# Expert numbers by steps, one-hots with stored pairs, and modulation vectors spread over the mixer's last stages

## The chip, the cores and the metric

The kernel runs on one core of one Trainium2 chip. The metric is the device time of one execution in microseconds (us), the median of several runs. All inputs and outputs lie in the chip's memory. One launch computes the whole trunk.

## The reference, cut to what matters

512 tokens of 1024 numbers pass through two layers. Each layer has a mixer (a gated linear recurrence HGRN2 in 8 heads beside a state space model S5, merged by gates) and an expert half, PEER. Both halves are entered through an RMS norm that is shifted and scaled by modulation vectors, and left through a modulated residual. All weights are float32.

```python
c_act = jax.nn.silu(c)
for l in range(DEPTH):                                   # 2
    mod = c_act @ ada_w[l] + ada_b[l]                    # 6 vectors of 1024
    sh1, sc1, g1, sh2, sc2, g2 = jnp.split(mod, 6, axis=-1)
    proj = modulate(rms_norm(x, norm1_g[l]), sh1, sc1) @ w_in[l]
    # q, f, i, og -> y_a (HGRN2); u -> y_s (S5, gelu); ga, gb: gates
    y_b = y_s * jax.nn.sigmoid(y_s @ glu_w[l] + glu_b[l])
    merged = jax.nn.sigmoid(ga) * y_a + jax.nn.sigmoid(gb) * y_b
    x = x + g1 * (merged @ w_out[l])
    h2 = modulate(rms_norm(x, norm2_g[l]), sh2, sc2)
    x = x + g2 * peer_layer(h2, ...)

# peer_layer, for every token and each of 8 heads:
s = jnp.einsum('thpd,hpnd->thpn', q, keys32)             # p = 2 halves, n = 128 keys
s1_v, s1_i = top_k(s[:, :, 0], 16); s2_v, s2_i = top_k(s[:, :, 1], 16)
cand_v = s1_v[..., :, None] + s2_v[..., None, :]         # 16 x 16 pairs
cand_i = s1_i[..., :, None] * 128 + s2_i[..., None, :]
top_v, top_j = top_k(cand_v, 16)
idx = take_along_axis(cand_i, top_j)                     # numbers of 16 experts of 16384
gate = softmax(top_v)
act = gelu(sum_d u_tab[idx] * h)                         # one dot product per chosen expert
out = sum_k gate * act * v_tab[idx]
```

## The kernel before

The activations lie transposed, `xT` [128, 8, 512]: channels on the partitions, tokens along the row. The order of the instructions on each engine is not the order of the text: a planner places every instruction by a priority (its place in the text, less an offset where a block asks for one) and by its own estimate of when operands and buffers are ready.

**A dense product** (`dense`, L125) multiplies 128 output channels by all tokens. Weight and activation are each split into a high part in TensorE's reduced float32 and the rest. `load_split` (L106) loads 512 KB on SP's queue into `raw` (4 buffers), ScalarE copies the high part `whi` (L114), VectorE subtracts to get `wlo` (L116), and 24 matmuls follow: 8 depth blocks times high-high (L132), high-low (L133) and low-high (L134). Activations are split once per stage by `split_act` (L119, VectorE's part L123). Weight splits of later products are put up to 1000 places ahead (`HP`).

**The mixer's last stages** (L727 to L777) are 32 dense products: 8 gates for the S5 branch (`gates`, two and then six), 8 gates for the HGRN2 branch (win columns 40 to 47), 8 products with `glu`, and 8 with `wout`, the last three of them in two halves of 256 tokens (`dense_halves`). Among them the modulation vectors are computed: `ada` (L160) takes chunks of 128 outputs; each is one load of 512 KB on SP into a tile with two buffers and one VectorE product with accumulation (L165), and one VectorE sum per call adds the bias. There are 48 chunks per layer. Of a layer's own chunks 16 to 47, one stands after each of the eight win stages (`later(1)`) and three before each glu stage (`later(3)`); before the first five wout stages of layer 0 stand chunks 0 to 15 of layer 1, four at a time (`later(4)`). `cond` loads c and computes its silu, in layer 1 just after the six gates.

**The expert half** (`peer`). `wq` gives 16 score blocks: `scores` (L812) copies the query, multiplies by the keys (L819, plain float32, 128x128) and takes the top 16 on VectorE. `select(tb)` (L826) works on a block of 128 tokens, one token per partition. It makes 50 candidate sums per head, those of the 16 x 16 pairs that can be among the top 16, with as many candidate numbers `ci`, and takes the top 16 and their positions `tj`. Then, for each of the 8 x 16 picks, one VectorE instruction (L855) compares a row of 0 to 49 with the position, multiplies by `ci` and accumulates the one number that is left; a shift and a mask split that number into the two key numbers `fx[0]` and `fx[1]`. The softmax gate is `fx[2]`.

The last 128 tokens fetch their experts one by one: `gather_steps` (L938) issues 128 indirect gathers of rows of U on POOL, with one VectorE dot product each (L946), and 128 of V, each added to `gacc` (L957), through three buffers `gr`.

The other 384 tokens use dense products over all 16384 experts. `dense_U` (L785) is a product with 128 experts, 24 matmuls of 384 columns, its gelu stored to memory; there are 128 per layer. The gate weights come from `build` (L886): for each token two matmuls (one for each part of the gate) of one-hot matrices [128 picks, 128 keys] puts the gates at their places in a 128 x 128 table. `select` transposes `fx` to picks on partitions and stores the two key numbers as float16 in `st` (`slot`) and the gate as a float16 high part and rest in `gh`, both with two buffers. One build takes 4 tokens: VectorE compares `io4` (a key number repeated four times) with four tokens' first and second key numbers (L900, L902), multiplies the second one-hot with the gate's two parts (L906, twice), all as [128, 128, 4] with the token as the innermost index; 8 matmuls follow (L912, L913), whose operands step over four elements; ScalarE copies to `stg` (L914), and every 12 builds `stg` goes to memory (`sW`).

```
    TE.matmul(ps[:, k], P_[:, :, t], Qs[0][:, :, t], start=True, stop=False)
    TE.matmul(ps[:, k], P_[:, :, t], Qs[1][:, :, t], start=False, stop=True)
```

In the text `select(3)` is first, then for each block of 0 to 2 its `select` and 32 builds, with one `dense_U` and one gather step after every second build, then the 80 remaining `dense_U` with a gather step each. After them comes the stage of V: for each of 128 groups of experts the stored gelu times the reloaded gates (L1007), a split (L1009, L1011), and 24 matmuls (L1020 to L1022) into eight accumulators, with the remaining gather steps between.

## Time and profile before

| what | value |
|---|---|
| median of three runs | 3928.33 us (3924.42 to 3931.42) |
| profiled execution's own time | 3930.45 us |
| its span | 3928.7 us, 62542 instructions |
| PE (TensorE) busy | 3736.3 us, 95% |
| PEld (weight loads, beside PE) | 3502.1 us, 89% |
| DVE (VectorE) busy | 3238.6 us, 82% |
| ACT (ScalarE) busy | 1574.6 us, 40% |
| POOL (GpSimd) busy | 1021.7 us, 26% |
| mean granted clock of TensorE | 0.97 |
| moved by DMA | 911.37 MB, 232 GB/s on the mean |

The span is the profiled part of one execution; 1.75 us lie around it. In time, layer 0's mixer heads take the first 450 us, the mixer's last stages 455 to 612, the score stage ends at 752, U and the builds run to 1435, V to 1965; layer 1 repeats this to the end. Busy shares are means over these stages. Clock and share are told as a part of one (1.00 is 2.4 GHz, 0.50 is 1.2 GHz). In a row, "out<-in" names the tiles written and read, and an arrow "<-" behind a wait names what ended it.

### The profile page before, as it was taken

To read this page: it belongs to the slowest core of one execution; us is meant where nothing else is said; L and a number is where in the kernel's file an instruction comes from. 1 tells how busy PE (TensorE), PEld (TensorE's weight loads), DVE (VectorE), ACT (ScalarE), POOL (GpSimd) and SP (SyncE) were. 2 spreads that over 40 slices of the span, in tenths; PEclk is the share of its full clock that TensorE was granted. 3 is DMA by queue.
4 is the path that set the end of the run, shared out by engine and by line. 5 is a ranking of instruction groups with operands and counts; after the bars stand their busy time and mean duration, and the time that the engine had idled before them with its cause. 6 is when DMAs were issued, how large, how long until landed. Compare 5 with 4: busy or idle time off the path is not lost.

```text
span 3928.7 us, 62542 instructions
## 1 busy us (share of the span) xinstructions
PE 3736.3 (95%) x21878; PEld 3502.1 (89%) x21878; DVE 3238.6 (82%) x8715; ACT 1574.6 (40%) x2507; POOL 1021.7 (26%) x1475
## 2 busy tenths in 40 slices
PE   6999999999999959999999999999999997699998
PEld 5888878999999959999988887789999997699998
DVE  6998787999898879877578886679998888787874
ACT  3554443333343323333345554344333433233332
POOL 7454100013222344221033440000232223432210
PEclk9999999999999969999999999999999998899999
DMA  5222384379998989998622225524898898999984
GB/s 197 74 64 78 102 266 143 111 249 318 326 315 304 322 300 351 348 344 315 208 85 75 71 81 168 187 84 136 303 309 315 310 325 289 333 353 344 347 294 134
DMA packets 368764, 911.37 MB, mean 232 GB/s; under 512 B 35824, under 2 KB 187440, under 8 KB 368448
## 3 DMA queue, kind: packets, MB, share of 16 engines
q1 hardware_dynamic: 247696, 536.56, 40.6%
q0 software_dynamic: 73952, 268.56, 19.7%
q10 hardware_dynamic: 46800, 102.26, 6.8%
q8 instruction: 172, 2.82, 0.3%
q14 instruction: 144, 1.18, 0.1%
HBM read 796.09 MB, written 111.15 MB: 231 GB/s over the span
## 4 chain that ended last, share of the span: by engine, by line
PE 77%; DVE 11%; DMA 7%; POOL 2%; issue 2%; ACT 1%; SPq 0%; ACTq 0%; DVEq 0%; POOLq 0%
PE mm L132 12%; PE mm L133 12%; PE mm L134 12%; PE mm L1021 3%; PE mm L1020 3%; PE mm L1022 3%; PE pb L1021 2%; PE pa L1022 2%; PE pb L1020 2%; PE pa L1021 2%; PE pa L1020 2%; PE pb L1022 2%; DMA ada<-ada 2%; DVE wlo L116 2%; PE pa L912 2%; PE pa L913 2%
## 5 line engine op out<-in xcount | busy, mean ns | idle before, releaser
L114 ACT ACTIVATE whi<-raw 128x1024 fp32r<-128x1024 f32 x688 | 728.4, 1060 | 1289.0 <-PE mm L133 751.2
L133 PE MATMUL mm<-alo,whi 128*128 128x384 f32 (+1 forms) x3360 | 1217.2, 363 | 13.6 <-DVE alo L123 13.5
L134 PE MATMUL mm<-ahi,wlo 128*128 128x384 f32 (+1 forms) x3360 | 1216.7, 363 | 10.5 <-DVE wlo L116 10.4
L132 PE MATMUL mm<-ahi,whi 128*128 128x384 f32 (+1 forms) x3360 | 1216.7, 364 | 10.5 <-ACT ahi L229 3.5
L116 DVE TENSOR_TENSOR wlo<-raw,whi 128x1024 fp32r<-128x1024 f32 x688 | 842.1, 1225 | 319.6 <-ACT whi L114 299.5
L133 PEld LDWEIGHTS mm<-alo,whi 128*128 128x128 f32 x3360 | 638.0, 190 | 63.7 <-DVE alo L123 14.8
L134 PEld LDWEIGHTS mm<-ahi,wlo 128*128 128x128 f32 x3360 | 638.1, 190 | 62.6 <-DVE wlo L116 14.0
L132 PEld LDWEIGHTS mm<-ahi,whi 128*128 128x128 f32 x3360 | 638.5, 190 | 61.6 <-ACT ahi L229 4.6
L936 POOL DMA_INDIRECT gr<-ur,idi x256 | 269.5, 1053 | 1481.4 <-DVE jk L855 764.6
L936 POOL DMA_INDIRECT gr<-v,idi x256 | 350.6, 1370 | 669.1 <-DVE gacc L957 583.0
L957 DVE SCALAR_TENSOR_TENSOR gacc<-gr,gate,gacc 128x1024 f32<-128x1024 f32 x254 | 324.5, 1277 | 45.3 <-DMA gr<-v,idi 45.0
L946 DVE SCALAR_TENSOR_TENSOR gr<-gr,rows 128x1024 f32<-128x1024 f32 x256 | 311.1, 1217 | 25.9 <-DMA gr<-ur,idi 24.2
L1021 PE MATMUL mm<-gl,whi 128*128 128x384 f32 x768 | 259.0, 338 | 0.7 <-DVE gl L1011 0.6
L1022 PE MATMUL mm<-gh,wlo 128*128 128x384 f32 x768 | 258.5, 337 | 0.0
L1020 PE MATMUL mm<-gh,whi 128*128 128x384 f32 x768 | 210.0, 338 | 50.6 <-ACT gh L1009 26.4
L1009 ACT ACTIVATE gh<-A 128x384 fp32r<-128x384 f32 x256 | 132.4, 518 | 296.7 <-DVE A L1007 257.8
L912 PE MATMUL pa<-Q,P 128*128 128x128 f16 x768 | 197.7, 296 | 45.2 <-DVE Q L906 42.9
L855 DVE SCALAR_TENSOR_TENSOR jk<-iof,tf,ci 128x50 f32<-128x50 f32 x1024 | 223.8, 262 | 0.0
L914 ACT ACTIVATE stg<-pa 128x512 f32<-128x512 f32 x192 | 114.0, 598 | 220.4 <-PE pa L913 192.2
L913 PE MATMUL pa<-Q,P 128*128 128x128 f16 x768 | 187.9, 295 | 0.9
L1020 PEld LDWEIGHTS mm<-gh,whi 128*128 128x128 f32 x768 | 140.6, 189 | 51.2 <-ACT gh L1009 51.2
L1020 PE MATMUL pb<-gh,whi 128*128 128x384 f32 x512 | 172.8, 338 | 0.0
(382 smaller groups left out, 6642.9 us busy)
## 6 DMA issues: line engine op xcount, KB each, us to landing
raw<-u SPq DMA_DIRECT2D x256, 512.0 KB
raw<-v SPq DMA_DIRECT2D x256, 512.0 KB
raw<-win SPq DMA_DIRECT2D x112, 512.0 KB
ada<-ada SPq DMA_DIRECT2D x96, 512.0 KB
sA<-uo ACTq DMA_DIRECT2D x256, 192.0 KB
sW<-stg ACTq DMA_DIRECT2D x64, 768.0 KB
A<-sA SPq DMA_DIRECT2D x256, 192.0 KB
W<-sW SPq DMA_DIRECT2D x64, 768.0 KB
```

What stands on the lines that cost most here:

```text
L114: S.activation(hi, raw, AF.Copy)
L116: V.tensor_tensor(lo, raw, hi[:].bitcast(F32), op=OP.subtract)
L132: TE.matmul(ps, hi[:, w], ah, start=(j == 0), stop=False)
L133: TE.matmul(ps, hi[:, w], al, start=False, stop=False)
L134: TE.matmul(ps, lo[:, w], ah, start=False, stop=(j == J - 1))
L912: TE.matmul(ps[:, k], P_[:, :, t], Qs[0][:, :, t], start=True, stop=False)
L936: G.indirect_dma_start(out=g[:], out_offset=None, in_=tab, in_offset=bass.IndirectOffsetOnAxis(ap=ids[:, s_:s_ + 1], axis=0))
L946: V.scalar_tensor_tensor(g, g, 1.0, rows, op0=OP.mult, op1=OP.mult, accum_out=dot[:, s_:s_ + 1])
L957: V.scalar_tensor_tensor(acc_, g, gate[:, s_:s_ + 1], acc_, op0=OP.mult, op1=OP.add)
L1020: TE.matmul(ps, w[0][:, c], g[0], start=first, stop=False)
L1021: TE.matmul(ps, w[0][:, c], g[1], start=False, stop=False)
L1022: TE.matmul(ps, w[1][:, c], g[0], start=False, stop=last)
```

## The change

Three parts.

*Expert numbers.* `ranks`, called for four heads at a time, replaces the 128 picks of L855 and the shift and mask. The row r of a candidate at position j is the number of row starts (`thr`, from COFF) at or below j, and the column is j less the lengths (`cnd`, from CAND) of the rows passed. So the first key number is the first one plus the sum, over r, of (j >= start of r) times the step between sorted key numbers r-1 and r, and the second is the sum over 16 columns of (column equals r2) times the second key number. All of it is float16 with two equal values stored beside each other, and sums are taken by halving. The small tables are filled once, in layer 0's mixer (`rank_tables`). The candidate numbers `ci` are no longer made.

*One-hots.* `io4` becomes `ioh`, the row of key numbers seen as 64 pairs. `st` and `gh` hold each value twice in a row, [128, 128, 2, 2], in one buffer each instead of two. A build compares both key numbers of four tokens in one instruction of 1024 elements, and multiplies in two of 512; one-hots now lie token by token, so the matmuls read them in a run.

*Modulation vectors.* One list of the 48 chunks (32 in layer 1, which has no next one) is spread evenly over 27 places: the six gates, the eight win stages, the eight glu stages and the first five wout stages. `ada` is called for one chunk at a time. `cond` of layer 1 stands ahead of the gates.

```diff
-    io4 = cst.tile([128, 128, 4], F16, name="io4")
-    V.tensor_copy(io4, it[:, :, None].to_broadcast([128, 128, 4]))
+    ioh = cst.tile([128, 64, 2], F16, name="ioh")
+    V.tensor_copy(ioh, it[:].rearrange("p (a b) -> p a b", b=2))
...
+    thr = cst.tile([128, 15, 2], F16, name="thr")
+    cnd = cst.tile([128, 15, 2], F16, name="cnd")
+    rnk = cst.tile([128, 16, 2], F16, name="rnk")
+
+    def rank_tables():
+        V.tensor_copy(rnk, iof[:, 0:16, None].to_broadcast([128, 16, 2]))
+        for r in range(1, 16):
+            G.memset(thr[:, r - 1], float(COFF[r]))
+            G.memset(cnd[:, r - 1], float(CAND[r - 1]))
...
         pk0 = pack_tile(fx)
+        if l == 0:
+            rank_tables()
...
-        gates(J - 2, fx)
         if l > 0:
             cond(fx, stp)
-        todo = list(range(16, 48))
-        follow = list(range(16)) if l + 1 < layers else []
-
-        def later(n, l_=l, todo=todo):
-            n = min(n, len(todo))
-            if n:
-                ada(l_, [todo.pop(0) for _ in range(n)], hp, "ada")
+        todo = [(l, i) for i in range(16, 48)] + [(l + 1, i) for i in range(16) if l + 1 < layers]
+        parts = 6 + 8 + 8 + 5
+        share = [len(todo) * (k + 1) // parts - len(todo) * k // parts for k in range(parts)]
+
+        def later():
+            for _ in range(share.pop(0)):
+                l_, i = todo.pop(0)
+                ada(l_, [i], hp, "ada")
+
+        for _ in range(J - 2):
+            gates(1, fx)
+            later()
...
-            later(1)
+            later()
...
-            later(3)
+            later()
...
-            later(4, l + 1, follow)
+            later()
             merge(e, dense(a["wout"][l, e], mg))
...
+        def ranks(iv, j, o0, o1):
+            j = j.rearrange("p h k -> p (h k)")
+
+            def work(n):
+                return rp.tile([128, T], F32, tag="s", name=nm("s"))[:].bitcast(F16)[:, 0:64 * n].rearrange(
+                    "p (r x) -> p r x", r=n)
+
+            def pairs(t, n):
+                return t[:, :, None, :].to_broadcast([128, n, 32, 2])
+
+            def twos(w):
+                return w.rearrange("p r (a b) -> p r a b", b=2)
+
+            def total(w, n, o):
+                while n > 2:
+                    m = (n + 1) // 2
+                    V.tensor_tensor(w[:, 0:n - m], w[:, 0:n - m], w[:, m:n], op=OP.add)
+                    n = m
+                V.tensor_tensor(o, w[:, 0], w[:, 1], op=OP.add)
+
+            def gate_rows(w, t, n):
+                sh = [128, n * 4, 8, 2]
+                v = w.rearrange("p r (h a b) -> p (r h) a b", h=4, b=2)
+                V.tensor_tensor(v, v, t[:].rearrange("p r h b -> p (r h) b")[:, :, None, :].to_broadcast(sh), op=OP.mult)
+
+            step = rp.tile([128, 15, 4, 2], F16, tag="step", name=nm("step"), bufs=1)
+            two = [128, 4, 15, 2]
+            V.tensor_tensor(step[:].rearrange("p r h b -> p h r b"), iv[:, :, 0, 1:16, None].to_broadcast(two),
+                            iv[:, :, 0, 0:15, None].to_broadcast(two), op=OP.subtract)
+            second = rp.tile([128, 16, 4, 2], F16, tag="second", name=nm("second"), bufs=1)
+            S.activation(second[:].rearrange("p r h b -> p h r b"), iv[:, :, 1, :, None].to_broadcast([128, 4, 16, 2]),
+                         AF.Copy)
+            ge, w = work(15), work(15)
+            V.tensor_tensor(twos(ge), twos(j[:, None].to_broadcast([128, 15, 64])), pairs(thr, 15), op=OP.is_ge)
+            V.tensor_tensor(twos(w), twos(ge), pairs(cnd, 15), op=OP.mult)
+            r2 = rp.tile([128, 64], F16, tag="r2", name=nm("r2"), bufs=1)
+            total(w, 15, r2)
+            V.tensor_tensor(r2, j, r2, op=OP.subtract)
+            gate_rows(ge, step, 15)
+            total(ge, 15, o0)
+            o0 = o0.rearrange("p (h k) -> p h k", h=4)
+            V.tensor_tensor(o0, o0, iv[:, :, 0, 0:1].to_broadcast([128, 4, 16]), op=OP.add)
+            eq = work(16)
+            V.tensor_tensor(twos(eq), twos(r2[:, None].to_broadcast([128, 16, 64])), pairs(rnk, 16), op=OP.is_equal)
+            gate_rows(eq, second, 16)
+            total(eq, 16, o1)
...
-            idf = rp.tile([128, 16, 16], F32, tag="idf", name=nm("idf"), bufs=1)
+            idf = rp.tile([128, 16, 16], F16, tag="idf", name=nm("idf"), bufs=1)
             V.tensor_copy(idf, sx[:, tb])
             idv = idf[:].rearrange("p (h s) k -> p h s k", s=2)
-            V.tensor_scalar(idv[:, :, 0, :], idv[:, :, 0, :], 128.0, None, op0=OP.mult)
             cv = rp.tile([128, 8, NCAND], F32, tag="cv", name=nm("cv"), bufs=1)
-            ci = rp.tile([128, 8, NCAND], F32, tag="ci", name=nm("ci"), bufs=1)
-            for src, dst in ((val, cv), (idv, ci)):
+            for src, dst in ((val, cv),):
...
-            tf = rp.tile([128, 8, 16], F32, tag="tf", name=nm("tf"), bufs=1)
-            V.tensor_copy(tf, tj)
-            code = rp.tile([128, 8, 16], F32, tag="code", name=nm("code"), bufs=1)
-            for hh in range(8):
-                for k in range(16):
-                    jk = rp.tile([128, NCAND], F32, tag="jk", name=nm("jk"))
-                    V.scalar_tensor_tensor(jk, iof[:, 0:NCAND], tf[:, hh, k:k + 1], ci[:, hh], op0=OP.is_equal,
-                                           op1=OP.mult, accum_out=code[:, hh, k:k + 1])
-            cint = rp.tile([128, 128], I32, tag="cint", name=nm("cint"), bufs=1)
-            V.tensor_copy(cint, code[:].rearrange("p h k -> p (h k)"))
-            ii = rp.tile([128, 2, 128], I32, tag="ii", name=nm("ii"), bufs=1)
-            V.tensor_scalar(ii[:, 0], cint, 7, None, op0=OP.logical_shift_right)
-            V.tensor_scalar(ii[:, 1], cint, 127, None, op0=OP.bitwise_and)
+            jf = rp.tile([128, 8, 16], F16, tag="jf", name=nm("jf"), bufs=1)
+            V.tensor_copy(jf, tj)
             fx = rp.tile([128, 3, 128], F32, tag="fx", name=nm("fx"), bufs=1)
-            V.tensor_copy(fx[:, 0:2], ii)
+            for hf in range(2):
+                ranks(idv[:, 4 * hf:4 * hf + 4], jf[:, 4 * hf:4 * hf + 4], fx[:, 0, 64 * hf:64 * hf + 64],
+                      fx[:, 1, 64 * hf:64 * hf + 64])
...
-            st = rp.tile([128, 2, 128], F16, tag="slot", name=nm("slot"))
-            S.activation(st, pt[:, 0:2], AF.Copy)
-            gh = rp.tile([128, 2, 128], F16, tag="gh", name=nm("gh"))
-            V.tensor_copy(gh[:, 0], pt[:, 2])
-            V.tensor_tensor(gh[:, 1], pt[:, 2], gh[:, 0], op=OP.subtract)
+            st = rp.tile([128, 128, 2, 2], F16, tag="slot", name=nm("slot"), bufs=1)
+            gh = rp.tile([128, 128, 2, 2], F16, tag="gh", name=nm("gh"), bufs=1)
+            for i in range(2):
+                S.activation(st[:, :, i], pt[:, i, :, None].to_broadcast([128, 128, 2]), AF.Copy)
+            g2 = pt[:, 2, :, None].to_broadcast([128, 128, 2])
+            V.tensor_copy(gh[:, :, 0], g2)
+            V.tensor_tensor(gh[:, :, 1], g2, gh[:, :, 0], op=OP.subtract)
...
-            sh = [128, 128, NT]
-
-            def row(t):
-                return t[:, None, :].to_broadcast(sh)
-
-            P_ = rp.tile(sh, F16, tag="P", name=nm("P"))
-            V.tensor_tensor(P_, io4, row(st[:, 0, c]), op=OP.is_equal)
-            Q_ = rp.tile(sh, F16, tag="Qo", name=nm("Qo"))
-            V.tensor_tensor(Q_, io4, row(st[:, 1, c]), op=OP.is_equal)
-            Qs = []
+            sh = [128, 2 * NT, 64, 2]
+
+            def pairs(t):
+                return t[:, c].rearrange("p t i b -> p (t i) b")[:, :, None, :].to_broadcast(sh)
+
+            PQ = rp.tile([128, NT, 2, 128], F16, tag="PQ", name=nm("PQ"))
+            V.tensor_tensor(PQ[:].rearrange("p t i (a b) -> p (t i) a b", b=2), ioh[:, None].to_broadcast(sh), pairs(st),
+                            op=OP.is_equal)
+            QQ = rp.tile([128, NT, 2, 128], F16, tag="QQ", name=nm("QQ"))
             for i in range(2):
-                q = rp.tile(sh, F16, tag=f"Q{i}", name=nm("Q"))
-                V.tensor_tensor(q, Q_, row(gh[:, i, c]), op=OP.mult)
-                Qs.append(q)
+                V.tensor_tensor(QQ[:, :, i].rearrange("p t (a b) -> p t a b", b=2),
+                                PQ[:, :, 1].rearrange("p t (a b) -> p t a b", b=2),
+                                gh[:, c, i, None].to_broadcast([128, NT, 64, 2]), op=OP.mult)
+
             for b in range(NT // 4):
                 ps = ptile([128, 4, 128], "pa")
                 for k in range(4):
                     t = 4 * b + k
-                    TE.matmul(ps[:, k], P_[:, :, t], Qs[0][:, :, t], start=True, stop=False)
-                    TE.matmul(ps[:, k], P_[:, :, t], Qs[1][:, :, t], start=False, stop=True)
+                    TE.matmul(ps[:, k], PQ[:, t, 0], QQ[:, t, 0], start=True, stop=False)
+                    TE.matmul(ps[:, k], PQ[:, t, 0], QQ[:, t, 1], start=False, stop=True)
```

## Rows read from the trace of the kernel before

**Rows 1.** Windows: length, busy (instructions) of PE, PEld, DVE, ACT, POOL; clock; DMA share; GB/s
```profile
752.00:1365.00 613.00, 610.53 (x3690) 594.58 (x3689) 563.36 (x2189) 242.87 (x352) 148.68 (x139) 1.00 0.86 296
1365.00:1435.00 70.00, 24.31 (x169) 18.44 (x167) 52.48 (x107) 13.77 (x24) 36.69 (x20) 0.51 0.81 286
1435.00:1965.00 530.00, 528.66 (x2992) 528.02 (x2993) 411.03 (x657) 192.18 (x252) 129.26 (x98) 0.99 0.89 315
3305.00:3375.00 70.00, 21.97 (x145) 17.02 (x144) 47.58 (x89) 12.33 (x21) 27.97 (x19) 0.50 0.79 280
```

**Rows 2.** Windows, instructions of L132 alone: PE, PEld
```profile
752.00:1365.00 613.00, 345.34 (x1021) 193.19 (x1021) 1.00 0.86 296
```

**Rows 3.** Timeline of PE around 750 us: start, length in us, instruction
```profile
749.59 1.05 PE L819 MATMUL pb<-key,q 128*128 128x128 f32 x8
750.39 0.42 PE L132 MATMUL mm<-ahi,whi 128*128 128x384 f32 x1
750.65 0.33 PE L133 MATMUL mm<-alo,whi 128*128 128x384 f32 x1
750.82 0.34 PE L134 MATMUL mm<-ahi,wlo 128*128 128x384 f32 x1
```

**Rows 4.** Windows, instructions of L912 alone: PE, PEld
```profile
752.00:1365.00 613.00, 77.27 (x300) 35.95 (x301) 1.00 0.86 296
1365.00:1435.00 70.00, 21.59 (x84) 10.04 (x83) 0.51 0.81 286
```

**Rows 5.** Timeline of PE around 1009 us, first and last of eight matmuls
```profile
1008.50 0.29 PE L912 MATMUL pa<-Q,P 128*128 128x128 f16 x1
...
1009.32 0.30 PE L913 MATMUL pa<-Q,P 128*128 128x128 f16 x1
```

**Rows 6.** Chain that ended last, 1365 to 1440 us: start, length, what
```profile
1367.55 1.34 DVE Q L906 x4
...
1411.47 0.61 ACT stg L914
...
1414.73 12.64 DMA sW<-stg
...
1435.64 1.31 PE mm L1020 x3
```

**Rows 7.** What PE waited for, 455 to 612 us: sum, times, longest
```profile
PE mm L133 <- DVE alo L123: 6.9, 2, 6.4
```

**Rows 8.** What PE waited for, 2395 to 2500 us, in layer 1
```profile
PE mm L133 <- DVE alo L123: 6.7, 1, 6.7
```

**Rows 9.** Chain that ended last, 485 to 610 us, shares by line
```profile
by line: DMA ada<-ada 33.9%; DVE ada L165 16.1%; DVE wlo L116 7.2%; issue 6.0%; PE mm L134 5.4%; PE mm L133 5.3%; PE mm L132 5.2%; DMA raw<-wout 3.3%; DVE alo L123 3.1%; ACT ysf L754 2.5%; DVE sg L765 2.5%; ACT L754 2.1%; ACT whi L114 1.5%;
```

**Rows 10.** Groups by line and shape, VectorE: busy, mean ns, idle before
```profile
L855 DVE SCALAR_TENSOR_TENSOR jk<-iof,tf,ci 128x50 f32<-128x50 f32 x1024 | 223.8, 262 | 0.0
...
L906 DVE TENSOR_TENSOR Q<-Qo,gh 128x512 f16<-128x512 f16 x384 | 145.9, 417 | 9.7 <-PE pa L912 9.7
...
L757 DVE TENSOR_TENSOR sgb<-sgb,ysf 128x512 f32<-128x512 f32 x16 | 11.1, 691 | 11.7 <-ACT ysf L754 11.7
```

**Rows 11.** The whole chain's longest pieces, one of L855
```profile
802.65 2.88 DVE jk L855 x30
```

**Rows 12.** L653 alone: shortest, median and longest in ns; first and last
```profile
L653 DVE TENSOR_TENSOR F<-F x96: 392/423/954, 78.5 to 2378.4; 128x256 f32<-128x256 f32 x96
```

**Rows 13.** Timeline of PE around 1399 us, seven matmuls from first to last
```profile
1399.39 0.30 PE L912 MATMUL pa<-Q,P 128*128 128x128 f16 x1
...
1400.10 0.29 PE L912 MATMUL pa<-Q,P 128*128 128x128 f16 x1
```

**Rows 14.** Windows, instructions on tile gr alone: DVE, POOL
```profile
1435.00:1965.00 530.00, 129.02 (x101) 129.26 (x98) 0.99 0.89 315
```

**Rows 15.** L957 alone: shortest, median and longest in ns; first and last
```profile
L957 DVE SCALAR_TENSOR_TENSOR gacc<-gr,gate,gacc x254: 1266/1277/1286, 1339.6 to 3782.3; 128x1024 f32<-128x1024 f32 x127
```

**Rows 16.** Timeline of POOL at the start, with its wait in brackets
```profile
22.18 1.34 POOL L286 TENSOR_TENSOR s5s<-s5s 128x32 f32<-128x32 f32 x2 [15.16 <-DMA s5s<-are]
```

## The prediction

> **What bounds the kernel now.** I read four views in this order: windows by stage, the counts of single lines in those windows, the timeline of TensorE (PE), and the chain that ended last. In each layer's expert half, from the first matmuls over the expert table U to the first over V, PE is busy 610.5 of 613 us at full granted clock, and VectorE (DVE) 563.4 of 613; then comes a stretch of 70 us in which PE does 24 us of work at the 1.2 GHz level while DVE does 52; layer 1 has the same hole [rows 1]. The reader is to see that PE is the bound up to 1365 us and DVE in the hole. The first follows from counts: 1021 of L132 [rows 2] is 1021 triples of matmuls at 0.173 us each [rows 3], 530 us, and 300 pairs from the builds [rows 4] at 2 x 0.117 us [rows 5], 70 us: 600 of 613. The second: 84 of the 384 pairs of one layer are left for the hole [rows 4], when U has nothing more to give, and in the chain the hole is DVE's build steps up to 1411.5, the store of the gate weights (12.6 us) and the way to the first matmul over V at 1435.6 [rows 6]. The stage of V is PE-bound again [rows 1]. In the mixers' last stages PE waits for a DVE split once per layer, 6.9 and 6.7 us [rows 7, 8], because a third of the chain there is loading modulation vectors [rows 9].
>
> **The change, part by part.** Times are summed against the profiled execution (3930.45 us; the median of the three runs shown is 2.1 lower).
>
> *Price of a packed step.* Four 512-element float16 steps in a row take 1.34 us, 0.335 each [rows 6]. A 512-element float16 step is recorded at 417 ns and a float32 one at 691 [rows 10]; if the difference, 274 ns, is what packing two elements saves, an element costs 0.535 ns packed and 1.07 not, and a step 0.061 us beside its elements.
>
> *Expert numbers.* Removed per select: 128 steps of L855 with their accumulator reads, 30 instructions in 2.88 us [rows 11], so 0.192 us a pair and 24.6 us; and twelve small instructions (the seven sums into ci, the product with 128, the casts and shifts), an estimate of 0.14 us each from that pair's two, 1.6 us. Added: 2 x 20 DVE steps. One half counts 7,928 elements: 20 x 0.061 + 7,928 x 0.535 ns = 5.5 us, 5.7 with the four that write float32. Each step needs the one before, and a record is 82 ns longer than a step; where nothing else stands between them that adds 1.6 us. So 11.4 to 14.6 us per select; I take 13, as other work mostly does stand between. The larger copies of the gates add 0.4. Saved: 12.8 per select, 51 per layer. ScalarE gets one copy more per half and is busy 243 of 613 us [rows 1].
>
> *One-hots on DVE.* Four steps of 0.335 become one of 1,024 elements (0.061 + 0.548) and two of 0.335: 1.28 for 1.34, 6 us over 96 builds. Unpacked they would cost 1.16 + 2 x 0.61 = 2.37, 99 us more; below, I see no gain beyond the 6. I take packed: the one row with an operand word held still, L653 (a float32 value repeated along the row), has a median of 423 ns at 256 elements [rows 12], where the price above plus 82 ns gives 0.061 + 0.274 + 0.082 = 417.
>
> [...]
>
> *One-hots on PE.* Eight build matmuls start 0.117 us apart [rows 5], and 0.118 at the 1.2 GHz level [rows 13]: the array's clock does not set this step. Float32 matmuls of the same 128 x 128 with operands stored in a run take 0.80/8 = 0.100 [rows 3], on twice the bytes. So I put the 0.117 down to reading float16 at a step of four elements; the change stores them in a run. Below: 0.173 x 128/384 = 0.058; above: 0.117, nothing gained. I take 0.075, nearer to the lower end, because the float32 row bounds it at 0.100 and moves twice the bytes. 768 x 0.042 = 32 us of PE per layer.
>
> [...]
>
> *What that moves.* PE: 752 + 530 + 768 x 0.075 = 1340 us for the last build, with U and builds without a hole. DVE: it does 563 + 52 = 616 us from 752 to 1435 [rows 1]; less 51 and 6 it is 559, and at today's 563/613 = 0.92 that takes 608 us: 1360. The later one counts, so DVE sets the last build, at 1360. Behind it stay the copy, the store and the reload, 1411.5 to 1435.6 = 24 us [rows 6]. V begins at 1384 instead of 1435.6: 52 us per layer, 103 for two (layer 1's hole is as long [rows 1]). What is late next is the gathers: 98 are left to V now [rows 14], and 52 us less before it leaves 15 more at the hole's 20 per 70 us. In layer 1 the last is added at 3782 [rows 15], while V runs from about 3375 to 3910: 15 more at (3782 - 3375)/98 = 4.2 us each end 63 us later, still hidden.
>
> *One buffer for slot numbers and gates.* ScalarE's copy into them now waits for the last build of the block before, twice per layer, and the conversions of U's weights stand behind it on ScalarE. Two further weight tiles of 4.2 us cover some 8 us; the planner orders the queues, so I cost it at nothing, and at 2 x 2 x 5 us if that cover fails.
>
> *Modulation vectors.* The same number of loads and products, but one or two per stage instead of three and four; 44 more single-column sums on DVE, beside PE's work; on SP each load now stands between weight loads, and in layer 1 the load of c moves ahead of the six gates. A stage of 24 matmuls of 512 columns takes an estimate of 5.5 us (4/3 of 0.173 each); in it 1.5 MB are loaded instead of 2.1 to 2.6. I take the two waits away, 13.6, rounded to 14 with the microseconds at half clock behind each; bounds 6 us worse (a load blocking a weight load once per layer) to 20 better.
>
> *Small set-up.* Thirty POOL fills at the start: POOL is idle 15.2 us there, waiting for the first S5 data [rows 16], so they cost nothing up to 0.5 us each.
>
> Sum: 3930 - 103 - 14 = 3813, against the median 3811.
>
> **The rivals.**
> *The matmul step stays 0.117.* Then PE ends the builds at 752 + 530 + 90 = 1372, V begins at 1396: 40 per layer. 3928 - 80 - 14 = 3834. For it: nothing in these rows shows float16 read in a run. Against: [rows 3, 13].
> *DMA becomes the bound.* Moved between 752 and 1965 in layer 0: 613 x 296 + 70 x 286 + 530 x 315 kB = 368 MB in 1213 us [rows 1], 304 GB/s on the mean; the forecast asks 317 of a memory that already runs at a share of 0.86 to 0.89. If it gives 310, 26 per layer is left: 3928 - 52 - 14 = 3862. The gathers are then what V waits for.
> *The hole closes wholly.* If the planner puts the last builds and the store ahead of the last U's, V begins with PE, 5 us after 1340: 90 per layer: 3928 - 180 - 14 = 3734.
> *Slower: pairs are not packed.* [...] Builds: +99 us of DVE per layer. Ranks: 7,928 x 1.07 ns + 1.2 = 9.7 per half, 19.4 a select, 6 saved instead of 12.8: 24 a layer. DVE has 616 + 99 - 24 = 691, at 0.92 751 us, V at 1527: 91 later per layer. 3928 + 182 - 14 = 4096. It decides from the point where a build costs 0.5 us more than today, where the ranks' saving is used up. [...]
>
> **How the numbers follow.** Chances: the forecast 0.44 (own range 3775 to 3848), the unchanged matmul step 0.18, DMA 0.12, the closed hole 0.20, unpacked pairs 0.06. The likeliest gives 3811. The range of 3720 to 3885 takes in the first four and leaves out unpacked pairs and the far ends of the others, about 0.15. A measurement of this kernel tells about 0.2%, 8 us, from no change. Faster by more needs a fourteenth of the sum: 0.92; within it 0.03, the far end of the DMA case; slower 0.05, the unpacked pairs less a part that the mixers and PE give back.
>
> **What would show it.** Right: the pair steps at about 0.61 and 0.335 us; build matmuls at under 0.1 us; some 12 to 15 us of new DVE work per select; V beginning 45 to 60 us earlier in its layer; no wait over 3 us for a split in the mixers' last stages; L957 still ending well before the last V matmuls. Wrong: a 1,024-element step at over 1 us; a hole of still 70 us, which would mean that DVE's load did not set it; or PE waiting within V.

## The result

The changed kernel takes 3864.5 us (median of four runs, 3857.2 to 3866.8) against 3929.4 us: a ratio of 0.9834 with a 95% interval of 0.9817 to 0.9851. It is faster by 65 us, 1.7%, clear of the noise. The forecast was 3811: it had almost twice the gain. The measured time lies within the stated range (3720 to 3885) and outside the forecast's own (3775 to 3848).

Where each layer's stages begin, from the two profiled executions (us); the last column is how much longer or shorter the stretch that ends there has become:

| | before | changed | difference of the stretch |
|---|---|---|---|
| first product over U, layer 0 | 750.4 | 749.6 | -0.8 (mixer) |
| first product over V, layer 0 | 1435.6 | 1393.0 | -41.8 (U and builds) |
| last scores, layer 1 | 2694.5 | 2654.4 | +2.5 (V, mixer) |
| first product over V, layer 1 | 3373.0 | 3292.6 | -40.3 (U and builds) |
| end of the span | 3928.7 | 3855.5 | +7.2 (V, final norm) |

So the stage of U and builds gave 82 of the 103 us forecast, the mixers nothing of 14. The profiled execution (3857.2 us) was the quickest of the four. Of the 7 us at the end 4.7 are in V's matmuls (539.9 us before, 544.6 now), where PE waits twice for the high part of a gelu (L1063), 2.9 us in all; before, it waited there only at V's start. In the row for 3292 to 3856 us the longest wait, 16.7 us, is the step into V:

```profile
PE mm L1074 <- ACT gh L1063: 19.6, 3, 16.7
```

Why these two come late stays open. The other 2.5 us lie behind V, as 2 to 3 us do in several kernels below.

The profile after. First the windows of layer 0 (columns as in [rows 1]):

```profile
752.00:1293.00 541.00, 523.19 (x3447) 501.64 (x3446) 487.02 (x1216) 230.96 (x349) 149.60 (x124) 0.99 0.86 307
1293.00:1373.50 80.50, 72.76 (x407) 72.44 (x406) 47.13 (x48) 24.95 (x36) 28.24 (x23) 0.94 0.92 337
1373.50:1393.00 19.50, 0.34 (x2) 0.02 (x1) 9.86 (x13) 1.96 (x3) 6.09 (x7) 0.58 0.95 329
```

The last build's matmul is at 1292.6, not at 1411 as before: the builds now run ahead of U, and 80 us of products over U stand behind them. The hole with half-speed builds in it is gone; what is left is 19.5 us in which PE does nothing. But PE, which was busy 610.5 of 613 us before, has new gaps. What PE waited for, over the whole span (sum, times, longest):

```profile
PE mm L142 <- ACT uo L804: 47.5, 15, 7.7
PE mm L1074 <- ACT gh L1063: 22.5, 5, 16.7
PE mm L1074 <- DMA s5s<-ldt: 19.2, 1, 19.2
...
PE mm L143 <- DVE alo L133: 12.1, 2, 7.4
```

The first row was 0.3 us before:

```profile
PE mm L132 <- ACT uo L788: 0.3, 1, 0.3
```

The next product over U waits for an accumulator, which waits for ScalarE's gelu, which waits for one of two buffers `uo` that is still being stored. The last row shown is the wait of [rows 7, 8], still there. The chain shows the first one at its longest:

```profile
1296.58 1.89 ACTq L972
...
1299.55 0.50 ACT uo L804 x2
1300.06 16.66 DMA sA<-uo
...
1316.74 0.50 ACT uo L804
...
1317.28 0.69 PE mm L142
1317.97 0.32 PE mm L143
...
1322.50 0.18 PE mm L143
```

A 192 KB store takes 16.66 us where the median is 4.9; just ahead of it on ScalarE's queue are the four pieces of a gate store (L972), 3 MB, the last of which lands at 1315.0, 1.7 us before it. In layer 0 there are eight such gate stores, and two stores of `uo` behind each take 13.6 to 19.0 us; of the others whose landing the trace has, none takes over 9.5. The matmuls after the wait are 0.32 us apart until 1322.1, at a granted clock of 0.50 (384 columns at 1.2 per ns, the prediction's 1.2 GHz level; at 1.00, from there on, 0.175 us and 2.2 per ns): the wait costs 7.7 us and some 2.2 more (15 matmuls at 0.32 instead of 0.175).

The prices that the forecast worked out, in the groups of DVE and the timeline of PE (answering [rows 10] and [rows 5]):

```profile
L958 DVE TENSOR_TENSOR QQ<-PQ,gh 128x512 f16<-128x512 f16 x384 | 142.9, 421 | 0.2
...
L954 DVE TENSOR_TENSOR PQ<-ioh,slot 128x1024 f16<-128x1024 f16 x192 | 127.7, 685 | 40.1 <-PE pa L967 39.7
...
L865 DVE TENSOR_TENSOR s<-s,second 128x1024 f16<-128x1024 f16 x16 | 10.9, 681 | 0.0
```

```profile
1004.46 0.23 PE L967 MATMUL pa<-QQ,PQ 128*128 128x128 f16 x1
1004.52 0.22 PE L966 MATMUL pa<-QQ,PQ 128*128 128x128 f16 x1
1004.58 0.22 PE L967 MATMUL pa<-QQ,PQ 128*128 128x128 f16 x1
```

A pair step of 1,024 elements is recorded at 685 ns, 0.603 us without the 82 ns that a record is longer (forecast 0.61), and build matmuls stand 0.055 us apart (0.117 before; forecast 0.075).

### The profile page after: what moved, and what is told of

Same layout as the page of the kernel before. It is cut to its first block, busy times and chain, and to the rows that moved or that the text cites. A ratio compares the mean times of both kernels' runs of the same rounds, so it can differ in the third digit from the quotient of the medians.

```text
span 3855.5 us, 60666 instructions
## 1 busy us (share of the span) xinstructions
PE 3670.2 (95%) x21878; PEld 3437.0 (89%) x21878; DVE 3113.5 (81%) x6744; ACT 1577.8 (41%) x2529; POOL 1044.4 (27%) x1505
## 4 chain that ended last, share of the span: by engine, by line
PE 66%; DMA 10%; issue 9%; DVE 8%; POOL 4%; ACT 2%; ACTq 0%; SPq 0%; POOLq 0%; DVEq 0%
PE mm L142 9%; PE mm L143 9%; PE mm L144 9%; PE mm L1075 4%; PE mm L1074 4%; PE mm L1076 3%; DMA sA<-uo 3%; POOL gr L990 3%; DMA ada<-ada 2%; PE pa L1076 2%; PE pb L1075 2%; PE pa L1075 2%; PE pb L1076 2%; PE pa L1074 2%; PE pb L1074 2%
## 5 line engine op out<-in xcount | busy, mean ns | idle before, releaser
L142 PE MATMUL mm<-ahi,whi 128*128 128x384 f32 (+1 forms) x3360 | 1225.2, 366 | 58.5 <-ACT uo L804 47.5
L142 PEld LDWEIGHTS mm<-ahi,whi 128*128 128x128 f32 x3360 | 641.2, 191 | 112.3 <-ACT uo L804 50.7
L990 POOL DMA_INDIRECT gr<-ur,idi x256 | 312.5, 1221 | 1417.0 <-DMA sA<-uo 727.8
L144 PEld LDWEIGHTS mm<-ahi,wlo 128*128 128x128 f32 x3360 | 639.9, 190 | 62.2 <-DVE wlo L126 13.6
L990 POOL DMA_INDIRECT gr<-v,idi x256 | 328.3, 1282 | 681.3 <-DVE gacc L1011 587.3
L1063 ACT ACTIVATE gh<-A 128x384 fp32r<-128x384 f32 x256 | 131.6, 518 | 241.4 <-DVE A L1061 202.1
L1074 PE MATMUL pa<-gh,whi 128*128 128x384 f32 x512 | 172.9, 338 | 0.0
L1076 PE MATMUL pa<-gh,wlo 128*128 128x384 f32 x512 | 172.3, 337 | 0.0
L1075 PE MATMUL pb<-gl,whi 128*128 128x384 f32 x512 | 172.2, 336 | 0.0
L1075 PE MATMUL pa<-gl,whi 128*128 128x384 f32 x512 | 172.1, 336 | 0.0
```

The costliest lines, as they stand in the source:

```text
L142: TE.matmul(ps, hi[:, w], ah, start=(j == 0), stop=False)
L144: TE.matmul(ps, lo[:, w], ah, start=False, stop=(j == J - 1))
L990: G.indirect_dma_start(out=g[:], out_offset=None, in_=tab, in_offset=bass.IndirectOffsetOnAxis(ap=ids[:, s_:s_ + 1], axis=0))
L1063: S.activation(gh, A, AF.Copy)
L1074: TE.matmul(ps, w[0][:, c], g[0], start=first, stop=False)
L1075: TE.matmul(ps, w[0][:, c], g[1], start=False, stop=False)
```

## The experiments

All times are medians beside runs of the kernel before on the same chip; not all kernels ran on one chip, so across rows the ratios compare better than the times. "Wait for uo" is PE's, over both layers. Two more kernels, further down, were run once each, for their traces alone.

| kernel | us | ratio (95%) | wait for uo | V begins, layer 0 |
|---|---|---|---|---|
| vectors spread, alone | 3928.8 | 0.9999 (0.9990 to 1.0008) | none | 1434.0 |
| expert numbers, alone | 3878.5 | 0.9868 (0.9853 to 0.9883) | 14.0 | 1422.3 |
| one-hots, alone | 3920.9 | 0.9979 (0.9968 to 0.9990) | 21.5 | 1429.5 |
| changed, four buffers uo | 3783.2 | 0.9630 (0.9613 to 0.9647) | none | 1366.2 |
| changed, pieces staggered in the text | 3863.3 | 0.9823 (0.9804 to 0.9841) | 50.7 | 1394.0 |
| changed, gates stored by SP | 3813.1 | 0.9696 (0.9679 to 0.9712) | 18.6 | 1381.7 |
| expert numbers, four buffers uo | 3856.9 | 0.9808 (0.9791 to 0.9824) | none | 1399.4 |
| four buffers, batches of 32 tokens | 3782.1 | 0.9628 (0.9610 to 0.9647) | none | 1357.5 |
| the same, W and A early | 3763.2 | 0.9579 (0.9554 to 0.9603) | none | 1351.5 |
| the same, four buffers for vectors | 3750.5 | 0.9537 (0.9524 to 0.9550) | none | 1341.0 |

### The parts alone

Each is the kernel before with the hunks of one part of the diff.

> The kernel before with the modulation vectors spread over the 27 places, and nothing else. Theory (from the trace of the changed kernel): no gain, within 4 us of before. With the vectors spread, TensorE still waits once per layer for the activation split ahead of wout or glu (7.4 and 4.7 us in the changed kernel, 6.9 and 6.7 before), since that wait is the chain from the last product of the stage before through sigmoid, product and split, not a load. Rival (the forecast): the loads of the vectors make that chain late; both waits go and the time falls by 14 us (ratio 0.9964).

The time did not move, as written, but for another reason. PE's wait for the split is 11.2 us over both layers (13.6 before). The chain before the longer of its two waits:

```profile
526.43 4.57 DMA ada<-ada
...
531.03 1.23 DVE ada L165 x2
532.26 0.60 DVE ya L751
532.87 0.61 DVE alo L123
...
533.52 0.80 PE mm L133
```

It is a load after all. On DVE the split (L123) stands behind the product of a vector (L165), and that product behind its load. The spread changed which vector this is, and not that there is one.

> The kernel before with the expert numbers by steps, and nothing else. Theory: VectorE's load set the hole between U and V, and the new numbers take about 51 us a layer off it, so V begins at about 1396 us (TensorE then ends U and builds at 752 + 530 + 90 = 1372, and some 24 us follow) and the time falls by 70 to 80 us, as much as by the whole change; TensorE waits little for the store of the gelus, since two builds at 0.117 us a matmul stand between two products over U. Rival: the gain comes from the shorter build matmuls, and this kernel alone gives 20 us or less.

It gave 49 us, less than expected and most of the whole change. The last build moved to 1293.1 as in the changed kernel, so DVE's load had set the hole; the last product over U came at 1400.6, later than the 1372 of the sum, with a part of the wait for uo already there (with four buffers, below, it is 1384).

> The kernel before with the one-hots as stored pairs and contiguous matmul operands, and nothing else. Theory: VectorE's load stays at 610 of 616 us, so the last build of a layer moves by no more than 6 us and the time by 0 to 15 us; the hole gets longer as U ends sooner. Build matmuls are 0.055 us apart. Rival: TensorE set the stage, its 47 us a layer come out at the end, and the time falls by 60 us or more.

It gave 8 us, as expected. The hole stayed (columns as in [rows 1]):

```profile
752.00:1355.00 603.00, 582.46 (x3671) 565.91 (x3669) 554.74 (x2106) 240.93 (x353) 166.42 (x139) 0.99 0.86 300
1355.00:1429.00 74.00, 27.17 (x189) 17.51 (x188) 57.70 (x95) 15.23 (x27) 32.80 (x22) 0.53 0.83 298
```

PE now has 20.5 us of idle time ahead of the hole (2.5 before), and DVE 58 us of work in it: PE got faster, was not the last one and so waited. The three parts alone add up to 60 us by the ratios, the whole is 65.

### The store of the gelus

```diff
-UB = 2
+UB = 4
```

> The changed kernel with four buffers in place of two for the gelu of U's products (uo). Theory (queue): the 192 KB stores of uo stand behind the 3 MB store of the gate weights on ScalarE's queue; each of these holds up one store by 15 to 20 us, and with two buffers and three accumulators TensorE waits some 5 us after each (47.5 us over both layers). With four buffers the wait falls below 10 us in sum, and the time is 30 to 45 us below the changed kernel's (3820 to 3835 us, ratio to before 0.972 to 0.976). Rival (bandwidth): memory gives no more than it did; other waits (for U's weights, for gathered rows) take the place of this one and the time falls by less than 12 us.

The wait is gone, and the kernel is 81 us faster than the changed one, well over the 30 to 45 expected. In the profiles the two stages of U are 27 and 36 us shorter (643 us to 616, and 638 to 602). Of these 63 us the wait is 47.5 and a shorter step to V is 6; the rest fits the time at half clock behind the waits (up to the last product over U the mean granted clock was 0.98, and is 1.00). Another 8 us are between the two stages, and 7 at the end, those that the changed kernel lost there. The rate rose with it:

```profile
752.00:1300.00 548.00, 539.57 (x3550) 519.56 (x3549) 496.19 (x1229) 234.86 (x357) 154.62 (x127) 1.00 0.88 313
1300.00:1351.00 51.00, 51.00 (x306) 50.74 (x305) 27.38 (x29) 18.58 (x27) 13.72 (x12) 1.00 0.95 345
```

In the last 51 us of products over U PE is busy throughout, at 345 GB/s. The stores did not get quicker; their time to landing (minimum, median, maximum of the window 1150 to 1300), first in the changed kernel, then with four buffers:

```profile
DMA to landing us min/median/max: 1.9/5.0/19.0
```
```profile
DMA to landing us min/median/max: 2.6/4.6/18.0
```

So more buffers hide the slow stores. Is it the queue that makes them slow, or the traffic? The first try to tell:

```diff
             if o + NT == SG:
-                for q in range(0, 128, 32):
-                    nc.scalar.dma_start(sW[l][n, :, q:q + 32], stg[0][:, q:q + 32])
+                sent.extend((n, stg[0], q) for q in range(0, 128, 32))
+            if sent:
+                store(4 if t0 + NT == TD else g8 % 2)
```

`store` issues so many pieces from the list, one after every second build in the text.

> The changed kernel, uo with its two buffers, but the four 768 KB pieces of each gate-weight store are issued two builds apart instead of at once (at once only for the last of a layer): same bytes, same queue. Theory (queue): a store of uo then stands behind one piece at most, TensorE's wait for uo falls from 47.5 us below 15, and the time is 3785 to 3810 us. Rival (bandwidth, or the number of buffers whatever the queue): the landings stay long since all traffic is the same, at least 30 us of the wait stay, and the time is 3850 us or more.

Nothing changed, and the timeline of ScalarE says why this is no verdict:

```profile
1211.32 3.78 ACTq L980 DMA_DIRECT2D sW<-stg  x4
...
1215.67 0.74 ACTq L805 DMA_DIRECT2D sA<-uo  x1
```

All four pieces were still issued within 3.8 us. They were ready when `stg` was, and the planner had put them together again, so this run says nothing of queue or traffic. The second try moves them to another queue:

```diff
-                    nc.scalar.dma_start(sW[l][n, :, q:q + 32], stg[0][:, q:q + 32])
+                    nc.sync.dma_start(sW[l][n, :, q:q + 32], stg[0][:, q:q + 32])
```

> The changed kernel, uo with its two buffers, but the stores of the gate weights go through SP's queue instead of ScalarE's. Theory (queue): the stores of uo then land in under 9 us each, TensorE's wait for uo (47.5 us) falls below 8, and the time is 3785 to 3830 us, the upper part if the loads of U's weights, now behind those stores on SP's queue, come late. Rival (bandwidth): the same bytes move at the same time, the stores of uo still take 12 us or more beside a store of the gates, 30 us or more of the wait stay, and the time is 3850 us or more.

The time lies in the theory's interval. The stores of uo in the same window now land in 9.3 us at most, as far as the trace has their landing (19 of 29; 25 of 27 in the changed kernel):

```profile
DMA to landing us min/median/max: 1.9/6.2/9.3
```

The same bytes move beside them, and PE's longest wait for uo fell from 7.7 to 3.3 us, so it was mainly the queue. On one queue, in the changed kernel's layer 0, the first store of uo behind each of the eight gate stores landed 1.7 to 7.3 us after the last piece of that store whose landing the trace has, and took up to 19.0 us; beside the gates, on another queue, 9.3 us is the most seen. The edit also frees ScalarE from issuing the four pieces (up to 1.89 us each, in the chain above), which the time to landing does not contain; how much of the wait that was is not separated. The wait fell from 47.5 to 18.6 us, not below 8 as expected; that the traffic has a share in what is left (median 6.2 against 5.0) is likely and not shown. The step from U to V did not get shorter: its wait is 21.5 us in layer 0, where it was 19.2 in the changed kernel and is 14.9 with four buffers. It ends with a load of W now:

```profile
PE mm L1074 <- DMA W<-sW: 21.5, 1, 21.5
```

That load is on the queue of the gates' stores, but not held up by them; the last four were issued 74 to 78 us before, and the median landing of such a piece is 10.8 us in this run:

```profile
1289.73 3.91 SPq L972 DMA_DIRECT2D sW<-stg  x4
1367.73 0.47 SPq L1059 DMA_DIRECT2D W<-sW  x1
```

### What the one-hots are worth with that wait covered

The kernel with expert numbers alone, and UB = 4.

> The kernel before with the expert numbers by steps and four buffers for uo; the one-hots and the modulation vectors as before. Theory: with uo covered the one-hots' shorter matmuls are worth what they free on TensorE, some 35 to 45 us a layer, since they then set when the last product over U ends; this kernel then takes 3850 to 3865 us, 70 to 80 above the changed kernel with four buffers (3783). Rival: the one-hots are worth what they brought with two buffers (3878 - 3864 = 14 us, or the 8 us alone) whatever the buffers, and this kernel takes 3790 to 3800 us.

It takes 3857 us. Against 3783 the one-hots (with the vectors, which gave nothing alone) are worth 74 us (70 by the ratios), where with two buffers they are worth 3878.5 - 3864.5 = 14. Layer 0 here:

```profile
752.00:1284.00 532.00, 528.71 (x3272) 508.79 (x3271) 470.22 (x1272) 222.06 (x332) 126.15 (x109) 1.00 0.82 289
1284.00:1384.00 100.00, 100.00 (x580) 100.00 (x578) 58.23 (x72) 34.83 (x50) 28.51 (x27) 1.00 0.94 335
```

PE is busy 628.7 us until its last product over U; with the one-hots and four buffers it is 539.6 + 51.0 = 590.6 until 1351. That is 38 us a layer, against the forecast's 32: the matmuls' gain was real, and in the changed kernel it was spent waiting. It is not 768 x 0.062 = 48, since only some 630 of a layer's 768 build matmuls follow another one directly.

### Which operand's step costs

PQ (the matmuls' weights) with the token innermost, and then QQ (their moving operand) so, each in the changed kernel:

```diff
-            PQ = rp.tile([128, NT, 2, 128], F16, tag="PQ", name=nm("PQ"))
+            PQ = rp.tile([128, 2, 128, NT], F16, tag="PQ", name=nm("PQ"))
```
```diff
-            QQ = rp.tile([128, NT, 2, 128], F16, tag="QQ", name=nm("QQ"))
+            QQ = rp.tile([128, 2, 128, NT], F16, tag="QQ", name=nm("QQ"))
```

> The changed kernel with PQ laid out with the token innermost, so that the build matmuls' weights are read at a step of four float16 elements and the moving operand QQ in a run (the compare is then four instructions of 256 elements, so VectorE's time is not to be compared). Theory A (the moving operand sets the step): build matmuls 0.055 to 0.06 us apart as in the changed kernel. Theory B (the weights set it): 0.117 us apart as before.

> The changed kernel with QQ laid out with the token innermost, so that the moving operand of the build matmuls is read at a step of four elements and the weights PQ in a run. Theory A: 0.117 us apart. Theory B: 0.055 to 0.06 us apart. If the step of 8 bytes does not matter at all, both kernels show 0.055.

Timelines of PE, the weights at a step of four first:

```profile
1013.09 0.22 PE L968 MATMUL pa<-QQ,PQ 128*128 128x128 f16 x1
1013.14 0.22 PE L967 MATMUL pa<-QQ,PQ 128*128 128x128 f16 x1
```
```profile
1006.75 0.30 PE L967 MATMUL pa<-QQ,PQ 128*128 128x128 f16 x1
1006.87 0.29 PE L966 MATMUL pa<-QQ,PQ 128*128 128x128 f16 x1
```

0.055 us apart with strided weights, 0.117 with a strided moving operand: theory A. The first rival (the step stays) is out: for a moving operand of float16 the step of 8 bytes made the 0.117. The two kernels as a whole are no gain (4209 and 4050 us, one run each); their DVE steps that write single elements take long: 772 ns for a compare of 256 with strided weights, 1345 for a product of 512 with a strided moving operand (the last section has the row).

### From the last product over U to the first over V

In the changed kernel this is 19.5 us in layer 0:

```profile
1374.66 0.48 ACT uo L804
1375.16 5.15 DMA sA<-uo
...
1380.40 0.33 SPq L1089
1380.77 0.43 SPq L1059
```

The loads of A (the stored gelus, L1089) and W (the stored gates, L1059) start when the last uo is stored: their tiles get memory that the stage of U holds until then. With UB = 4, and gates stored in batches of 32 to make room, they get memory of their own:

```diff
-SG = 48
+SG = 32
-                wt[0] = vp.tile([128, TD // SG, WG, SG], F32, tag="W", name=nm("W"), bufs=2)
+                wt[0] = gp.tile([128, TD // SG, WG, SG], F32, tag="W", name=nm("W"), bufs=2)
-            A = vp.tile([128, TD], F32, tag="A", name=nm("A"), bufs=3)
+            A = gp.tile([128, TD], F32, tag="A", name=nm("A"), bufs=3)
```

> The changed kernel with four buffers for uo, the tiles W and A of the stage of V in memory of their own, not in that of the stage of U, and, to make room, stored gates in batches of 32 tokens instead of 48. Theory: the first loads of V wait only since their memory is released by the last store of uo (1380.3 us in the changed kernel, V at 1393.0); with their own memory they land early, V begins within 4 us of the last product over U, and the time is 20 to 30 us below that with four buffers alone (3753 to 3763 us). Rival: the load of the first gelus waits for all of its table in memory to be stored, and the time stays within 8 us of 3783.

> The changed kernel with four buffers for uo and stored gates in batches of 32 tokens, W and A back in the memory of the stage of U's successor: the kernel with early W and A (3763 us) less that one step. Theory: the step from the last product over U to the first over V is 15 us again in both layers and the time is 3775 to 3783 us, so the early tiles are worth 12 to 20 us. Rival: the batches of 32 are what gained, the time is 3768 us or less.

The control takes 3782.1 us and the early tiles 3763.2: 19 us from them, none from the batches (3783 with four buffers alone). PE's wait ahead of the first product over V, control first:

```profile
1357.53 1.33 PE L1074 MATMUL mm<-gh,whi 128*128 128x384 f32 x3 [16.52 <-DMA s5s<-aim]
```
```profile
1351.50 1.33 PE L1074 MATMUL mm<-gh,whi 128*128 128x384 f32 x3 [6.45 <-ACT gh L1063]
```

6.45 us are left, not under 4 as expected; gh, the gelus' high part, still lies in the released memory, which may be why. That wasn't tried.

### The vectors once more

```diff
-            t = pool.tile([128, D], F32, tag=tag, name=nm("ada"), bufs=RAWB if tag == "raw" else 2)
+            t = pool.tile([128, D], F32, tag=tag, name=nm("ada"), bufs=RAWB if tag == "raw" else 4)
```

> The kernel with four buffers for uo and early W and A (3763 us), with four buffers in place of two for the loads of modulation vectors. The wait for the split (12.1 us over both layers there) ends with VectorE, in whose order the split stands behind a product of a modulation vector that itself waits for its load. Theory A (two buffers: each load starts only when the product two before is done): with four, loads run ahead, the wait falls below 5 us and the time by 8 to 16 us. Theory B (the mixers' last stages are bound by what memory gives to weights and vectors together): the loads only wait elsewhere, the wait stays above 9 us and the time within 5 us.

Theory A. What PE waited for, first before this edit and then with it:

```profile
PE mm L143 <- DVE alo L133: 12.1, 2, 6.2
```
```profile
PE mm L143 <- DVE alo L133: 3.2, 3, 1.2
```

At 3750.5 us this is the fastest version, 114 us below the changed kernel.

## Why the prediction was right, and where it was not

**Prices.** They held: 0.603 us for a pair step of 1,024 elements (0.61) and 421 ns recorded for 512 (417), so 1.28 us for a build's three steps. The 40 steps of a select for the expert numbers are recorded at 14.5 us together, 11.2 without the 82 ns of each (forecast 11.4 to 14.6). The rival of unpacked pairs is out: it had 1.16 us for the step of 1,024 and 2.37 for a build. The matmul step came out at 0.055, under the 0.075 taken. PE's relief was 38 us a layer, not 32.

**The step that failed** is "The later one counts, so DVE sets the last build, at 1360." It took all of DVE's work up to V as work that the last build has to wait for. With cheaper builds the planner ran them ahead: DVE did 487 us of work in 541 and the last build was at 1292.6; of splits and gathered rows some were left for later, 47 us of DVE's work beside the last products over U. V then hangs on the last product over U, not on the last build. By the forecast's own sum PE would be there at 1340; with the wait covered it was 1351, and in the changed kernel 1373.5. With the measured 0.055 that sum is 1324; it leaves out the changes between products and builds, the transposes of `select` and the 8 us in which PE waits (548 less 539.6). So the order of work that came was that of the rival "the hole closes wholly", the last builds ahead of the last products over U. It put V at 1345; with the wait covered V began at 1366, after a step of 15 us where the rival had 5.

**What was late next** was sought among the gathers. It was the store of the gelus behind the store of the gates, on a queue that the forecast did not look at, since PE waited 0.3 us for it before. The trace of before had the sign: ScalarE waited 39.9 us for these stores there, which PE did not feel:

```profile
L788 ACT ACTIVATE uo<-mm 128x384 f32<-128x384 f32 x256 | 121.1, 475 | 53.9 <-DMA sA<-uo 39.9 <-issue 5.6 <-PE pa L913 5.5
```

Products over U that follow each other faster use up the same two buffers sooner: PE's wait for uo was 0.3 us before, 14.0 with the expert numbers alone, 21.5 with the one-hots alone, 47.5 in the changed kernel. V began 9 us later than forecast in layer 0, and the stage of layer 1 gained 40 us instead of 52.

**The modulation vectors** were priced at 14 us and gave 0 (-4 to +3). The forecast read the loads' share of the chain [rows 9] rightly as the cause of the waits, but took fewer vectors in a stage to be the remedy. What mattered was that two buffers let no load run ahead; four gave 13 us (16 by the ratios). Four buffers without the spread were not tried.

**The rival "DMA becomes the bound"** has the measured time, 3862, and is wrong: it held memory to 310 GB/s on the mean from 752 us to the end of V. In the changed kernel that mean is 314, and with four buffers it is 322:

```profile
752.00:1895.00 1143.00, 1119.67 (x6851) 1099.09 (x6850) 960.89 (x1938) 448.84 (x638) 321.16 (x256) 0.99 0.90 322
```

A number that fits is not a mechanism that fits. That holds for the forecast too, and some luck was in it: the range was wide enough for the time because it took in this rival. With the wait covered the same kernel takes 3783, 28 us below the forecast; the unforeseen wait then took 81.

**The signs.** The steps' prices, the build matmuls under 0.1 us and the work per select came as listed. V began 42.6 us earlier in layer 0, not 45 to 60, and the longest wait for a split stayed at 7.4 us, not under 3. Of the signs of being wrong a small part came: PE waits within V, four times 1.4 us.

**Right besides:** one buffer for slot numbers and gates costs nothing that the trace shows; the last V row is added at 3726, well before the last products.

## What to carry to other kernels

When an engine's load is cut, do not ask when its whole work is done, but which instruction the next stage waits for, and what the planner will let slip behind. A wait of 40 us on an engine that is not the bound is a warning: look at each small buffer that is emptied through a queue with large stores in it before making the consumer faster. And a part that is worth 8 us alone can be worth over 70 once what eats it is gone, here DVE's load and the wait, so test parts both ways: each alone, and the whole without each.

## What was not expected of the hardware

The moving operand of a float16 matmul of 128 columns takes 0.117 us at a step of 8 bytes and 0.055 in a run; weights at the same step cost nothing that shows (0.055). At the step it is 0.118 also in the hole before, at a granted clock of 0.51 [rows 1, 13], while in a run the matmuls follow the clock: in the hole that the one-hots alone leave, at 0.53, they are 0.106 us apart.

```profile
1361.04 0.31 PE L915 MATMUL pa<-QQ,PQ 128*128 128x128 f16 x1
1361.15 0.31 PE L914 MATMUL pa<-QQ,PQ 128*128 128x128 f16 x1
1361.26 0.31 PE L915 MATMUL pa<-QQ,PQ 128*128 128x128 f16 x1
```

DVE writing single float16 elements at that step took 1345 ns for 512 elements, over three times the 421 of the same product written in a run (its row is among the prices in the result). The row of the kernel with the strided moving operand:

```profile
L958 DVE TENSOR_TENSOR QQ<-PQ,gh 128x512 f16<-128x512 f16 x384 | 470.2, 1345 | 0.4
```
